# Holding the tokens of a two-layer trunk by parity from the SSD output on, with one 512-column score tile a block of queries

## The chip, the cores and the metric

The kernel runs on one core of a Trainium2 chip. TensorE (PE, with its weight loader PEld) multiplies, VectorE (DVE) and ScalarE (ACT) do the elementwise work, and SyncE (SP) issues the DMAs. The metric is the device time of one execution in microseconds. Before the change it is 1275.34 us, the median of 3 runs from 1275.26 to 1276.29 us. Beside the runs there is the profile of one execution.

## The reference

256 tokens of width 2048 go through two layers; all data are float32. Each layer computes `x <- LayerNorm(alpha * x + (1 + gate) * mixer(x * (1 + scale) + shift))`, where shift, scale and gate come from a condition vector.

- The first mixer is a state-space one (SSD): a projection, a causal convolution of width 4, a scan over the tokens, a SiLU gate, an RMS norm over each of 8 groups of 512 channels, and an output projection from 4096 to 2048. Its output, normalised, also gives one set of keys and values.
- The second mixer is attention with 3 groups of 8 heads of width 128. The groups have windows and dilations (128, 1), (512, 4) and (2048, 16): a query at token t sees the keys t, t - d, t - 2d and so on, down to t - window. Each score is scaled and has a slope times the distance subtracted. The three groups' outputs are merged for each head slot by the weights of their softmax denominators, which is one softmax over the keys of all three groups. A SiLU gate and an output projection from 1024 to 2048 follow.

With 256 tokens, a key in the groups of dilation 4 and 16 is at an even distance from its query.

## The kernel before

Tokens lie in two blocks of 128, `b` = 0 and 1, the first and the second half of the sequence. A projection splits each weight piece of 512 KB into a high and a low part: ACT copies the high one (`split`, line 95) and DVE subtracts the low one (line 97), so that three fast matmuls (or two, in `cm_wide`, lines 145 and 148) make up a float32 product. The attention's own matmuls are plain float32, which TensorE runs as two instructions each.

The order is: the SSD layer (to about 535 us); its output projection in four chunks of 512 columns (`tm_chunk(wout[n], ...)`); keys and values (`cm_wide(wk...)`, `tm_chunk(wv...)`); then `queries(0)`, `attend(0)`, `queries(1)`, `attend(1)`, `z_gate` for two halves of the heads, and the last projection with the final norm. The code is written in program order, and the framework's scheduler puts the instructions of each engine in an order of their own at build time, so that the attention's matmuls stand between those of the next projection. Each engine then runs its instructions in that order.

What the change and the prediction touch:

- `y_tiles` (line 654): while the first chunk of the output projection runs, it transposes the SSD output `y` (token rows) into channel rows, two tiles of 256 tokens to one PSUM bank `pt`. ACT writes the high part into `yhi`, with the norm's weight as scale (line 663), and DVE the low part into `ylo` (line 664). There are 32 such tiles.
- The residual (line 728): the rows of `x` for a block are loaded as `xr`, 128 rows of 512 columns.
- `attend` (line 840): for each of 4 heads and each block `b` of queries, and for each of the 3 groups, one score matmul against the keys of block 0 alone (`b` = 0, 128 columns) or of both blocks (`b` = 1, 256 columns) into a tile `aux` (2 buffers; line 850). DVE makes the bias from slope, distance and mask (line 852) and adds it to the scaled score in `sc0` or `sc1` (line 854). Then come the maximum (line 856), the exponential with its sum on ACT (line 858), the reciprocal and the scaling on DVE (lines 859 and 860), and transposes of the weights in blocks of 128 into PSUM tiles `po` (2 buffers; line 864), which ACT (groups 0 and 2, line 870) or DVE (group 1, line 868) copies into `pT`. After both blocks, six matmuls add up the head's output in another `po` tile (lines 873 and 874), which line 875 copies over the queries of group 0.
- `bias`, a table of 1024 columns: 256 of distances and 3 x 256 of masks.
- `store` (line 947), which writes the output's rows, 512 columns at a time.

Of the kernel before, what the change touches and what calls it, by code (L numbers as in the profile page):

```python
# [9 lines left out]
F32 = mybir.dt.float32  # L10
# [32 lines left out]

CI, CT, CM, NCONST = 0, 128, 256, 640

CD, CA, NBIAS = 0, 256, 256 + 768


@with_exitstack
def trunk(ctx, tc, xT, x, c, par, cst, bias, lnrow, ada, wdt, win, wout, wk, wv, wbin, wbout, out):  # L50
# [32 lines left out]
    ones = cons.tile([P, P], F32, name="ones")  # L83
    V.memset(ones, 1.0)


    def load_piece(src):
        raw = wp.tile([P, 1024], F32, name="raw", bufs=6)
# [197 lines left out]
    with ExitStack() as cA:  # L286
# [367 lines left out]
        def y_tiles(g):  # L654

            for i in range(4):
                ct = 4 * g + i
                if i % 2 == 0:
                    pt = aux.tile([P, 512], F32, name="aux").rearrange("p (i l) -> p i l", i=2)
                for b in range(2):  # L660
                    T.transpose(pt[:, i % 2, b * P:b * P + P], y[g][:, b, i * P:i * P + P], ident)
                w, hi = pv("normg")[:, ct:ct + 1], yhi[g // 4][:, ct % 16, :]
                S.activation(hi, pt[:, i % 2, :], AF.Copy, scale=w)  # L663
                V.scalar_tensor_tensor(ylo[g][:, i, :], pt[:, i % 2, :], w, hi.bitcast(F32),
                                       op0=ALU.mult, op1=ALU.subtract)

        def y_ahead(q):
            if q == 0:
# [45 lines left out]
        for n in range(4):  # L714
            ps = tm_chunk(wout[n], lambda kt: yhi[kt // 16][:, kt % 16, :], lambda kt: ylo[kt // 4][:, kt % 4, :],
                          nk=2 * KT, rate=(1, 4) if n else (0, 1),
                          pre={0: y_ahead, 3: first_weights}.get(n), split_end=4 if n == 3 else 0)
            if n == 0:
                pin[0] = latest[-3].ins
                state[0] = 0  # L720
                queue(pn, cols1[:11])
            if n == 3:
                drain()
            gt = pn.tile([P, 512], F32, name="gt")
            bcast(gt, gated[0], 512 * n)
            for b in range(2):
                xr = pn.tile([P, 512], F32, name="xr", bufs=2)
                nc.sync.dma_start(xr, x[b * P:b * P + P, 512 * n:512 * n + 512])
                residual(n, ps[b], b, (gt, u[b][:, 512 * n:512 * n + 512]), xr)
                if n == 3:  # L730
                    norm.append(moments(b, 4))
                    normalise(b, 0, 256)
                    normalise(b, 256, 512)
# [78 lines left out]
    aux2 = ctx.enter_context(tc.tile_pool(name="aux3", bufs=2, space=PSUM))  # L812
    bs = pc2.tile([P, NBIAS], F32, name="bs", bufs=1)
    nc.sync.dma_start(bs, bias)
    dmat = bs[:, CD:CD + 256]
    amask = bs[:, CA:CA + 768].rearrange("p (g k) -> p g k", g=3)
    R = (0, 1)

    def weigh(n, b, i):
        if b == 0 and i == 0:  # L820
            t = pc2.tile([P, NG, 384], F32, name="pT", bufs=1).rearrange("p g n -> p (g n)")
            lnr[n] = [t[:, 512 * j:512 * j + 512] for j in range(2)]
            for j in range(2):
                bcast(lnr[n][j], lnrow, j * D + 512 * n)
        cs_ = slice(512 * n, 512 * n + 512)
        with tc.issue_after(late):
            V.tensor_tensor(u[b][:, cs_], u[b][:, cs_], lnr[n][i], op=(ALU.mult, ALU.add)[i])
# [12 lines left out]
    def attend(hq, qq):  # L840

        for i in range(4):
            h = 4 * hq + i
            pT = pc2.tile([P, NG, 384], F32, name="pT", bufs=1)
            for b in range(2):
                n = P * (b + 1)
                sc = pc2.tile([P, NG, n], F32, name=f"sc{b}", bufs=1)
                for g in range(NG):
                    pq = aux.tile([P, 512], F32, name="aux")[:, :n]
                    T.matmul(pq, qq[g][:, i, b * P:b * P + P], kv[hq, g][:, i, :n], start=True, stop=True)  # L850
                    bi = pc2.tile([P, 256], F32, name="bi", bufs=2)[:, :n]
                    V.scalar_tensor_tensor(bi, dmat[:, 256 - n:], SLOPES[g * H + h], amask[:, g, 256 - n:],
                                           op0=ALU.mult, op1=ALU.add)
                    V.scalar_tensor_tensor(sc[:, g, :], pq, SCALE, bi, op0=ALU.mult, op1=ALU.add)
                nm = sm.tile([P, 1], F32, name="nm")
                V.tensor_reduce(nm, sc, axis=AX.XY, op=ALU.max, negate=True)
                den = sm.tile([P, 1], F32, name="den")
                S.activation(sc, sc, AF.Exp, bias=nm, accum_out=den)
                V.reciprocal(den, den)
                V.tensor_scalar(sc, sc, den, None, op0=ALU.mult)  # L860
                for g in range(NG):
                    pp = aux2.tile([P, 512], F32, name="po")[:, :n]
                    for kb in range(b + 1):
                        T.transpose(pp[:, kb * P:kb * P + P], sc[:, g, kb * P:kb * P + P], ident)

                    d = pT[:, g, 0:P] if b == 0 else pT[:, g, P:384]
                    if g == 1:
                        V.tensor_copy(d, pp)
                    else:
                        S.activation(d, pp, AF.Copy)  # L870
            po = aux2.tile([P, 512], F32, name="po")[:, :L]
            for g in range(NG):
                T.matmul(po, vt[hq, g][:, 0, i * P:i * P + P], pT[:, g, 0:256], start=g == 0, stop=False)  # L873
                T.matmul(po[:, P:L], vt[hq, g][:, 1, i * P:i * P + P], pT[:, g, 256:384], start=False, stop=g == NG - 1)
            V.tensor_copy(qq[0][:, i, :], po)

    oghi, oglo = ([slots.tile([P, 4, L], F32R, name=f"s{2 * hq + i}") for hq in range(2)] for i in range(2))
# [16 lines left out]
    def hold_in(i, k):  # L894

        j = 4 + 2 * i + k
        if j < 12:
            return (slots if j < 8 else pb).tile([P, 1024], F32R, name=("s" if j < 8 else "b") + str(j))
        if i == 5:
            return pc2.tile([P, 1024], F32R, name="q2")  # L900
        return pc2.tile([P, 1024 + 128 * k], F32R, name=("bs", "pT")[k], bufs=1)[:, :1024]

    qs = [queries(0)]
    attend(0, qs[0])
# [40 lines left out]
        return end  # L945

    def store(b, c):
        nc.sync.dma_start(out[b * P:b * P + P, c], u[b][:, c])

    diag = pc2.tile([P, NG, P], F32, name="sc0", bufs=1)[:, 0, :]  # L950
    for n in range(2):
        last(0, n)
        join(2 + n, ps[n][0], 0)
# [57 lines left out]
def _layout(x, c, ada_w, ada_b, ln_g, ln_b, a_in_w, a_conv_w, a_conv_b, a_dt_bias,  # L1011
            a_A_log, a_D, a_norm_g, a_out_w, kv_w, b_in_w, b_out_w):
    f = np.float32
    par = np.zeros((P, NPAR), f)

    def put(name, a):
        par[:a.shape[0], OFF[name][0]:OFF[name][1]] = a

    ab = ada_b.reshape(2, 3, KT, P)
    put("adab", ab.transpose(3, 0, 2, 1).reshape(P, 96))  # L1020
    put("convw", a_conv_w[0].T.reshape(48, P, 4).transpose(1, 0, 2).reshape(P, 192))
    put("convb", _cm(a_conv_b[0]))
    put("normg", _cm(a_norm_g[0]))
    put("dsk", np.broadcast_to(a_D[0], (P, 64)))
    put("dtb", a_dt_bias[0][:, None])
    put("alog", np.broadcast_to(a_A_log[0], (P, 64)))
    put("lng", _cm(ln_g[0]))
    put("lnb", _cm(ln_b[0]))

    cst = np.zeros((P, NCONST), f)  # L1030
    i = np.arange(P)
    cst[:, CI:CI + 128] = np.eye(P)
    up = (i[:, None] <= i[None, :]).astype(f)
    cst[:, CT:CT + 128] = up
    cst[:, CM:CM + 384] = np.concatenate([up, up, np.ones((P, P), f)], 1)
    bias = np.zeros((P, NBIAS), f)
    delta = 128 + i[:, None] - np.arange(256)[None, :]
    bias[:, CD:CD + 256] = -delta
    for g, (win_, dil) in enumerate(((128, 1), (512, 4), (2048, 16))):
        ok = (delta >= 0) & (delta % dil == 0) & (delta <= win_)  # L1040
        bias[:, CA + 256 * g:CA + 256 * g + 256] = np.where(ok, 0.0, NEG)


    ada = ada_w.reshape(2, D, 3, KT, P).transpose(0, 2, 3, 4, 1)

    w = a_in_w[0]
    z, xs, bb, cc, dt = (w[:, a:b] for a, b in ((0, 4096), (4096, 8192), (8192, 9216), (9216, 10240), (10240, 10304)))
    bc = np.stack([bb.reshape(D, G, P), cc.reshape(D, G, P)], 2).reshape(D, 2048)
    win = _pieces(np.concatenate([bc, xs, z], 1))
    return {  # L1050
        "xT": x[0].T.reshape(KT, P, L).transpose(1, 0, 2), "x": x[0], "c": c, "par": par, "cst": cst, "bias": bias,
        "lnrow": np.stack([ln_g[0], ln_b[0], ln_g[1], ln_b[1]]),
        "ada": ada, "wdt": _dt(dt), "win": win,
        "wout": _pieces(a_out_w[0]), "wk": _pieces(kv_w[:, :3072], 256, 4),
        "wv": _pieces(kv_w[:, 3072:]), "wbin": _pieces(b_in_w[0], 256, 4), "wbout": _pieces(b_out_w[0]),
    }
# [20 lines left out]
```

## Time and profile before

| | |
|---|---|
| median of 3 runs | 1275.34 us |
| span of the profiled execution | 1272.5 us |
| instructions | 19056 |
| HBM read, written | 332.47 MB, 2.18 MB |
| granted TensorE clock, mean | 1.000 |

The span goes from the first to the last instruction of the program; the runs' times also hold what lies around it. In the profile's rows L850 is line 850 of the kernel. A group of instructions shows its line, engine and operation, the tiles written and read by their names in the program, the shape, the count, the busy time, the mean duration of one in ns, and the idle time of the engine just before them with what ended it. Matmuls are pipelined, so that the next one starts before the duration of the last is over. A wait is written as "who <- whom: total us, times, longest us".

### The profile page before, as it was taken

The page shows a single profiled execution, that of the slowest core. Times are in us where ns is not written, and L with a number is a line of the kernel's source. Part 1 is how long each engine was busy: PE and PEld are TensorE (multiplying, and loading weights), DVE is VectorE, ACT ScalarE, POOL GpSimd, SP SyncE. Part 2 cuts the span into 40 slices and gives each one's busy share as a digit, 9 for nine tenths or more (in the row PEclk, how much of TensorE's full clock was granted, in tenths as well). Part 3 has the DMA queues.
Part 4 walks back from the last instruction along what each step waited for, and adds up shares of the span by engine and source line. Part 5 has one row for each costly group of instructions (what it writes and reads, how often), then busy time and mean ns, then how long its engine had stood idle before and what let it go on. Part 6 is the DMA issues. An engine that isn't in the chain of part 4 may idle for free.

```text
span 1272.5 us, 19056 instructions
## 1 busy us (share of the span) xinstructions
PE 1236.6 (97%) x7222; PEld 1078.7 (85%) x7222; DVE 1034.5 (81%) x1498; ACT 704.0 (55%) x1035; POOL 0.2 (0%) x4
## 2 busy tenths in 40 slices
PE   4999999999999999999999999999999999999997
PEld 4889989899898999778888788888878888888885
DVE  6999986999998878869776678878888867758876
ACT  3655577757677777764344445434345645444731
POOL 0000000000000000000000000000000000000000
PEclk9999999999999999999999999999999999999999
DMA  9999968696866546468988469989998774463751
GB/s 386 423 420 422 420 211 298 224 341 234 314 247 208 157 149 216 167 216 292 338 282 282 160 195 353 357 328 348 357 381 316 235 240 130 127 204 100 222 192 66
DMA packets 80588, 335.89 MB, mean 264 GB/s; under 512 B 9105, under 2 KB 9329, under 8 KB 67697
## 3 DMA queue, kind: packets, MB, share of 16 engines
q1 hardware_dynamic: 80496, 334.69, 73.5%
q8 instruction: 56, 0.92, 0.3%
q14 instruction: 36, 0.29, 0.1%
HBM read 332.47 MB, written 2.18 MB: 263 GB/s over the span
## 4 chain that ended last, share of the span: by engine, by line
PE 85%; DVE 8%; DMA 3%; issue 2%; ACT 1%; SPq 0%; DVEq 0%; ACTq 0%
PE acc L145 14%; PE acc L171 12%; PE acc L170 12%; PE acc L169 12%; PE acc L148 7%; PE acc L123 7%; PE acc L121 7%; PE acc L122 7%; DVE araw L247 2%; DVE wlo L97 2%; PE py L608 2%; PE aux L850 1%; DMA araw<-in_ada 1%; DMA raw<-in_wk 1%; PE po L873 1%
## 5 line engine op out<-in xcount | busy, mean ns | idle before, releaser
L95 ACT ACTIVATE whi<-raw 128x1024 fp32r<-128x1024 f32 x392 | 411.3, 1058 | 369.4 <-PE acc L171 127.3
L97 DVE TENSOR_TENSOR wlo<-raw,whi 128x1024 fp32r<-128x1024 f32 x392 | 473.3, 1220 | 140.3 <-ACT whi L95 139.5
L145 PE MATMUL acc<-actT,whi 128*128 128x512 f32 x896 | 285.9, 398 | 0.0
L170 PE MATMUL acc<-wlo,actT 128*128 128x512 f32 x688 | 269.7, 392 | 1.1 <-DVE wlo L97 0.9
L169 PE MATMUL acc<-whi,actT 128*128 128x512 f32 x688 | 266.7, 394 | 0.9 <-ACT actT L663 0.9
L121 PE MATMUL acc<-actT,whi 128*128 128x256 f32 x768 | 217.4, 285 | 17.5 <-ACT actT L398 17.3
L247 DVE SCALAR_TENSOR_TENSOR araw<-araw,cb__72 128x2048 f32<-128x2048 f32 x96 | 219.2, 2284 | 14.6 <-DMA araw<-in_ada 14.5
L123 PE MATMUL acc<-actT,wlo 128*128 128x256 f32 x768 | 214.9, 285 | 4.9 <-DVE wlo L97 4.9
L122 PE MATMUL acc<-actT,whi 128*128 128x256 f32 x768 | 217.1, 284 | 0.0
L148 PEld LDWEIGHTS acc<-actT,wlo 128*128 128x128 f32 x896 | 167.0, 188 | 42.1 <-DVE wlo L97 5.0
L148 PE MATMUL acc<-actT,wlo 128*128 128x256 f32 x896 | 180.9, 282 | 1.9 <-DVE wlo L97 1.2
L171 PE MATMUL acc<-whi,actT 128*128 128x512 f32 x432 | 168.7, 391 | 0.0
L121 PEld LDWEIGHTS acc<-actT,whi 128*128 128x128 f32 x768 | 147.7, 193 | 18.7 <-ACT actT L398 17.5
L170 PEld LDWEIGHTS acc<-wlo,actT 128*128 128x128 f32 x688 | 129.3, 188 | 29.1 <-DVE wlo L97 3.4
L123 PEld LDWEIGHTS acc<-actT,wlo 128*128 128x128 f32 x768 | 146.5, 193 | 6.0 <-DVE wlo L97 5.8
L169 PEld LDWEIGHTS acc<-whi,actT 128*128 128x128 f32 x688 | 128.7, 188 | 26.7 <-ACT actT L663 1.4
L122 PEld LDWEIGHTS acc<-actT,whi 128*128 128x128 f32 x768 | 148.1, 193 | 0.3
L145 PEld LDWEIGHTS acc<-actT,whi 128*128 128x128 f32 x896 | 137.5, 189 | 0.3
L171 PE MATMUL acc<-whi,ylo 128*128 128x512 f32 x256 | 100.5, 393 | 0.0
L171 PEld LDWEIGHTS acc<-whi,actT 128*128 128x128 f32 x432 | 81.1, 188 | 16.6
L171 PEld LDWEIGHTS acc<-whi,ylo 128*128 128x128 f32 x256 | 48.0, 188 | 9.7
L319 DVE SCALAR_TENSOR_TENSOR cacc<-acc,prm,cacc 128x253 f32<-128x253 f32 (+2 forms) x96 | 42.1, 474 | 6.1 <-ACT cacc L316 5.8
(251 smaller groups left out, 1110.2 us busy)
## 6 DMA issues: line engine op xcount, KB each, us to landing
araw<-in_ada SPq DMA_DIRECT2D x96, 1024.0 KB, 7.5
raw<-in_win SPq DMA_DIRECT2D x160, 512.0 KB, 5.6
raw<-in_wout SPq DMA_DIRECT2D x64, 512.0 KB, 4.8
raw<-in_wbin SPq DMA_DIRECT2D x64, 512.0 KB, 4.3
raw<-in_wv SPq DMA_DIRECT2D x48, 512.0 KB, 5.4
raw<-in_wk SPq DMA_DIRECT2D x48, 512.0 KB, 7.7
cbc<-cumd SPq DMA_DIRECT2D x16, 512.0 KB, 5.2
raw<-in_wbout SPq DMA_DIRECT2D x16, 512.0 KB, 4.7
```

Of the source, the lines that this page charges most:

```text
L95: copied.append(S.activation(hi, raw, AF.Copy))
L97: latest.append(V.tensor_tensor(lo, raw, hi.bitcast(F32), op=ALU.subtract))
L121: T.matmul(o, hi[:, k, c_], ahi[:, kt, :], start=first, stop=False, skip_group_check=True)
L122: T.matmul(o, hi[:, k, c_], alo[:, kt, :], start=False, stop=False, skip_group_check=True)
L123: T.matmul(o, lo[:, k, c_], ahi[:, kt, :], start=False, stop=kt == k1 - 1, skip_group_check=True)
L145: T.matmul(ps[n], hi[:, k, n * P:n * P + P], xp[:, kt], start=kt == 0, stop=False, skip_group_check=True)
L148: T.matmul(ps[n][:, 0, :], lo[:, k, n * P:n * P + P], xhi[:, kt, :], start=False, stop=kt == KT - 1, skip_group_check=True)
L169: T.matmul(o, h_, hi[:, k, :], start=kt == k0, stop=False, skip_group_check=part)
L170: T.matmul(o, h_, lo[:, k, :], start=False, stop=False, skip_group_check=part)
L171: end = T.matmul(o, l_, hi[:, k, :], start=False, stop=kt == k1 - 1, skip_group_check=part)
L247: V.scalar_tensor_tensor(raw, raw, 1.0, cb_, op0=ALU.mult, op1=ALU.mult, accum_out=mod[layer][:, ct, j:j + 1])
L319: V.scalar_tensor_tensor(acc[:, o:], ps[:, :L - o], w[:, j:j + 1], acc[:, o:], op0=ALU.mult, op1=ALU.add)
```

## The change

Three things change.

First, `y_tiles` writes `yhi` and `ylo` with the tokens sorted by parity: columns 0 to 127 are the even tokens and 128 to 255 the odd ones. The transposes into PSUM stay as they are; the two copies read them with a step of two. From there on a "block" is a parity, down to the output: the residual's rows of `x` are loaded, and the output's rows stored, with a step of two rows (`rows`).

Second, in `attend` the groups of dilation 4 and 16 take keys of the query's own parity alone, 128 of them, and the group of dilation 1 takes all 256. So both blocks of queries have 256 + 128 + 128 columns of scores, in one PSUM bank; three matmuls fill it and one addition adds the bias. The biases are made once a head, for both blocks, in one tile `bi` of 640 columns (384 for group 0, whose two blocks take two different thirds of each side, and 128 for each of the others). The four transposes of a block go into one `po` tile, of which ACT copies the first half and DVE the second. The output is six matmuls, two of 256 columns and four of 128.

Third, the `bias` table has 384 columns of distances and 640 of masks, and some tiles have other sizes (`pT` 1024 columns in place of 1152, `sc0` and `sc1` 512 in place of 384 and 768).

```diff
-                w, hi = pv("normg")[:, ct:ct + 1], yhi[g // 4][:, ct % 16, :]
-                S.activation(hi, pt[:, i % 2, :], AF.Copy, scale=w)
-                V.scalar_tensor_tensor(ylo[g][:, i, :], pt[:, i % 2, :], w, hi.bitcast(F32),
-                                       op0=ALU.mult, op1=ALU.subtract)
+                w = pv("normg")[:, ct:ct + 1]
+                hi, lo = (t.rearrange("p (r j) -> p r j", r=2) for t in (yhi[g // 4][:, ct % 16, :], ylo[g][:, i, :]))
+                by_parity = pt[:, i % 2, :].rearrange("p (j r) -> p r j", r=2)
+                S.activation(hi, by_parity, AF.Copy, scale=w)
+                V.scalar_tensor_tensor(lo, by_parity, w, hi.bitcast(F32), op0=ALU.mult, op1=ALU.subtract)
...
+    def rows(t, b):
+        return t.rearrange("(j r) n -> r j n", r=2)[b]
...
-                nc.sync.dma_start(xr, x[b * P:b * P + P, 512 * n:512 * n + 512])
+                nc.sync.dma_start(xr, rows(x, b)[:, 512 * n:512 * n + 512])
...
-            pT = pc2.tile([P, NG, 384], F32, name="pT", bufs=1)
+            pT = pc2.tile([P, 4, 2, P], F32, name="pT", bufs=1)
+            bi = pc2.tile([P, 640], F32, name="bi", bufs=1)
+            for g, c_ in enumerate((slice(0, 384), slice(384, 512), slice(512, 640))):
+                V.scalar_tensor_tensor(bi[:, c_], dmat if g == 0 else dmat[:, P:2 * P], SLOPES[g * H + h], gmask[:, c_],
+                                       op0=ALU.mult, op1=ALU.add)
             for b in range(2):
-                n = P * (b + 1)
-                sc = pc2.tile([P, NG, n], F32, name=f"sc{b}", bufs=1)
-                for g in range(NG):
-                    pq = aux.tile([P, 512], F32, name="aux")[:, :n]
-                    T.matmul(pq, qq[g][:, i, b * P:b * P + P], kv[hq, g][:, i, :n], start=True, stop=True)
-                    bi = pc2.tile([P, 256], F32, name="bi", bufs=2)[:, :n]
-                    V.scalar_tensor_tensor(bi, dmat[:, 256 - n:], SLOPES[g * H + h], amask[:, g, 256 - n:],
-                                           op0=ALU.mult, op1=ALU.add)
-                    V.scalar_tensor_tensor(sc[:, g, :], pq, SCALE, bi, op0=ALU.mult, op1=ALU.add)
+                sc = pc2.tile([P, 512], F32, name=f"sc{b}", bufs=1)
+                pq = aux.tile([P, 512], F32, name="aux")
+                qb = slice(b * P, b * P + P)
+                T.matmul(pq[:, 0:L], qq[0][:, i, qb], kv[hq, 0][:, i, :], start=True, stop=True)
+                for g in range(1, NG):
+                    T.matmul(pq[:, (g + 1) * P:(g + 2) * P], qq[g][:, i, qb], kv[hq, g][:, i, qb], start=True, stop=True)
+                two = "p (a n) -> p a n"
+                bias_b = (bi[:, P:640].rearrange(two, a=2) if b == 0 else
+                          bass.AP(tensor=bi.tensor, offset=bi.offset, ap=[bi.ap[0], [384, 2], [1, 256]]))
+                V.scalar_tensor_tensor(sc.rearrange(two, a=2), pq.rearrange(two, a=2), SCALE, bias_b,
+                                       op0=ALU.mult, op1=ALU.add)
...
-                for g in range(NG):
-                    pp = aux2.tile([P, 512], F32, name="po")[:, :n]
-                    for kb in range(b + 1):
-                        T.transpose(pp[:, kb * P:kb * P + P], sc[:, g, kb * P:kb * P + P], ident)
-
-                    d = pT[:, g, 0:P] if b == 0 else pT[:, g, P:384]
-                    if g == 1:
-                        V.tensor_copy(d, pp)
-                    else:
-                        S.activation(d, pp, AF.Copy)
+                pp = aux2.tile([P, 512], F32, name="po")
+                for k in range(4):
+                    T.transpose(pp[:, k * P:k * P + P], sc[:, k * P:k * P + P], ident)
+                pp = pp.rearrange("p (k n) -> p k n", k=4)
+                S.activation(pT[:, 0:2, b, :], pp[:, 0:2, :], AF.Copy)
+                V.tensor_copy(pT[:, 2:4, b, :], pp[:, 2:4, :])
             po = aux2.tile([P, 512], F32, name="po")[:, :L]
-            for g in range(NG):
-                T.matmul(po, vt[hq, g][:, 0, i * P:i * P + P], pT[:, g, 0:256], start=g == 0, stop=False)
-                T.matmul(po[:, P:L], vt[hq, g][:, 1, i * P:i * P + P], pT[:, g, 256:384], start=False, stop=g == NG - 1)
+            head = slice(i * P, i * P + P)
+            for b in range(2):
+                T.matmul(po, vt[hq, 0][:, b, head], pT[:, b].rearrange("p b n -> p (b n)"), start=b == 0, stop=False)
+            for g in range(1, NG):
+                for b in range(2):
+                    T.matmul(po[:, b * P:b * P + P], vt[hq, g][:, b, head], pT[:, g + 1, b, :], start=False,
+                             stop=g == NG - 1 and b == 1)
...
-        nc.sync.dma_start(out[b * P:b * P + P, c], u[b][:, c])
+        nc.sync.dma_start(rows(out, b)[:, c], u[b][:, c])
```

More of the change, by code (lines that the diff above doesn't have):

```diff
@@ L44 @@
 CI, CT, CM, NCONST = 0, 128, 256, 640
-CD, CA, NBIAS = 0, 256, 256 + 768
+CD, CG, NBIAS = 0, 384, 384 + 384 + 256
 @with_exitstack
@@ L814, in trunk @@
     nc.sync.dma_start(bs, bias)
-    dmat = bs[:, CD:CD + 256]
-    amask = bs[:, CA:CA + 768].rearrange("p (g k) -> p g k", g=3)
+    dmat = bs[:, CD:CD + 384]
+    gmask = bs[:, CG:CG + 640]
     R = (0, 1)
@@ L820, in weigh @@
         if b == 0 and i == 0:
-            t = pc2.tile([P, NG, 384], F32, name="pT", bufs=1).rearrange("p g n -> p (g n)")
+            t = pc2.tile([P, 1024], F32, name="pT", bufs=1)
             lnr[n] = [t[:, 512 * j:512 * j + 512] for j in range(2)]
@@ L843, in attend @@
             h = 4 * hq + i
-            pT = pc2.tile([P, NG, 384], F32, name="pT", bufs=1)
-            for b in range(2):
-                n = P * (b + 1)
-                sc = pc2.tile([P, NG, n], F32, name=f"sc{b}", bufs=1)
-                for g in range(NG):
-                    pq = aux.tile([P, 512], F32, name="aux")[:, :n]
-                    T.matmul(pq, qq[g][:, i, b * P:b * P + P], kv[hq, g][:, i, :n], start=True, stop=True)
-                    bi = pc2.tile([P, 256], F32, name="bi", bufs=2)[:, :n]
-                    V.scalar_tensor_tensor(bi, dmat[:, 256 - n:], SLOPES[g * H + h], amask[:, g, 256 - n:],
-                                           op0=ALU.mult, op1=ALU.add)
-                    V.scalar_tensor_tensor(sc[:, g, :], pq, SCALE, bi, op0=ALU.mult, op1=ALU.add)
+            pT = pc2.tile([P, 4, 2, P], F32, name="pT", bufs=1)
[3 more added lines that the diff above has]
+                                       op0=ALU.mult, op1=ALU.add)
+            for b in range(2):
+                sc = pc2.tile([P, 512], F32, name=f"sc{b}", bufs=1)
[9 more added lines that the diff above has]
+                                       op0=ALU.mult, op1=ALU.add)
                 nm = sm.tile([P, 1], F32, name="nm")
-                V.tensor_reduce(nm, sc, axis=AX.XY, op=ALU.max, negate=True)
+                V.tensor_reduce(nm, sc, axis=AX.X, op=ALU.max, negate=True)
                 den = sm.tile([P, 1], F32, name="den")
@@ L900, in hold_in @@
             return pc2.tile([P, 1024], F32R, name="q2")
-        return pc2.tile([P, 1024 + 128 * k], F32R, name=("bs", "pT")[k], bufs=1)[:, :1024]
+        return pc2.tile([P, 1024], F32R, name=("bs", "pT")[k], bufs=1)
     qs = [queries(0)]
@@ L947, in store @@
     def store(b, c):
-        nc.sync.dma_start(out[b * P:b * P + P, c], u[b][:, c])
-    diag = pc2.tile([P, NG, P], F32, name="sc0", bufs=1)[:, 0, :]
+        nc.sync.dma_start(rows(out, b)[:, c], u[b][:, c])
+    diag = pc2.tile([P, 512], F32, name="sc0", bufs=1)[:, :P]
     for n in range(2):
@@ L1036, in _layout, with mask @@
     bias = np.zeros((P, NBIAS), f)
[L1037 to L1041, printed above, removed]
+    same = 2 * (i[:, None] - i[None, :])
+    near = np.concatenate([same + 1, same, same - 1], 1)
+    bias[:, CD:CD + 384] = -near
+    def mask(delta, win_, dil):
+        return np.where((delta >= 0) & (delta % dil == 0) & (delta <= win_), 0.0, NEG)
+    bias[:, CG:CG + 384] = mask(near, 128, 1)
+    bias[:, CG + 384:CG + 512] = mask(same, 512, 4)
+    bias[:, CG + 512:CG + 640] = mask(same, 2048, 16)
     ada = ada_w.reshape(2, D, 3, KT, P).transpose(0, 2, 3, 4, 1)
```

## The prediction

> **What bounds the kernel now.** I read the page first: the share of each engine and the chain that ended last. Then I read the stage that the change cuts, with the busy time by stretch, the waits of TensorE's weight loader and the rows in order of time.
>
> ```profile
> span 1272.5 us, 19056 instructions
> PE 1236.6 (97%) x7222; PEld 1078.7 (85%) x7222; DVE 1034.5 (81%) x1498; ACT 704.0 (55%) x1035; POOL 0.2 (0%) x4
> ...
> PE 85%; DVE 8%; DMA 3%; issue 2%; ACT 1%; SPq 0%; DVEq 0%; ACTq 0%
> ```
>
> TensorE is busy for 97% of the span and is 85% of the chain. The profiled execution has a span of 1272.5 us; the median of the runs is 1275.34, so 2.8 us lie around the span. I make the sum against the span and add those 2.8 us again.
>
> The attention is interleaved with projections: `attend(0)` with the matmuls of `queries(1)`, `attend(1)` with those of `z_gate`. Here are the stretches from the first score matmul to the last gate projection (us, then busy us of PE, its loader, DVE, ACT, POOL, the granted clock, the DMA share and rate):
>
> ```profile
> 1062.00:1110.00 48.00, 48.00 (x289) 41.45 (x288) 39.51 (x101) 25.00 (x49) 0.00 (x0) 1.00 0.36 105
> 1110.00:1150.00 40.00, 40.00 (x232) 34.94 (x231) 21.27 (x22) 17.44 (x21) 0.00 (x0) 1.00 0.68 206
> 1150.00:1216.00 66.00, 66.00 (x394) 56.76 (x393) 57.01 (x118) 41.28 (x70) 0.00 (x0) 1.00 0.55 169
> ```
>
> PE has no visible gap in 154 us; DVE has 36 us free and ACT 70. The loader's waits from 995 to 1216 us (total, times, longest):
>
> ```profile
> PEld po L864 <- ACT pT L870: 4.0, 13, 0.4
> PEld acc L148 <- DVE wlo L97: 0.7, 1, 0.7
> PEld po L864 <- DVE sc L860: 0.2, 1, 0.2
> ```
>
> Only the transposes wait, for a `po` buffer that a copy must empty, and only 0.3 us a time. The long softmax chain costs TensorE 0.2 us in all. So this stage is a sum of TensorE's own work.
>
> A matmul's duration overlaps the next one's, so I price by start to start:
>
> ```profile
> 1071.62 0.60 PE L864 MATMUL po<-cc,sc 128*128 128x128 f32 x4
> 1072.05 0.60 PE L850 MATMUL aux<-s,q 128*128 128x256 f32 x2
> 1072.48 0.43 PE L864 MATMUL po<-cc,sc 128*128 128x128 f32 x2
> ...
> 1073.49 0.60 PE L873 MATMUL po<-pT,s 128*128 128x256 f32 x2
> 1073.92 0.38 PE L874 MATMUL po<-pT,s 128*128 128x128 f32 x2
> 1074.14 0.60 PE L873 MATMUL po<-pT,s 128*128 128x256 f32 x2
> ```
>
> Four transposes take 0.43 us. One 256-column float32 matmul is two instructions and takes 0.43 (L850 and L873 alike); one of 128 columns takes 0.22. So a unit, one instruction of 128 columns, is 0.108 us.
>
> How much stall is in the stage? It begins at the first row below and ends at the last; between are 26 groups of projection matmuls without attention:
>
> ```profile
> 995.32 0.62 PE L145 MATMUL acc<-actT,whi 128*128 128x512 f32 x2
> ```
> ```profile
> 1193.69 0.62 PE L145 MATMUL acc<-actT,whi 128*128 128x512 f32 x2
> ...
> 1211.80 0.40 PE L145 MATMUL acc<-actT,whi 128*128 128x512 f32 x1
> ```
> ```profile
> 1215.98 0.40 PE L169 MATMUL acc<-whi,s 128*128 128x512 f32 x1
> ```
> ```profile
> L145 PE MATMUL acc<-actT,whi 128*128 128x512 f32 x512 | 165.3, 400 | 0.0
> ...
> L864 PE MATMUL po<-cc,sc 128*128 128x128 f32 x72 | 14.2, 281 | 0.0
> L850 PE MATMUL aux<-s,q 128*128 128x256 f32 x40 | 11.1, 379 | 0.0
> ```
>
> The stage is 1215.98 - 995.32 = 220.7 us. A group (two of L145, two of L148) takes (1211.80 - 1193.69) / 26 = 0.697 us, and 512 of L145 make 256 groups: 178.3 us. That leaves 42.4 us for attention. By the code a head has score matmuls of 3 x 128 and 3 x 256 columns, two instructions each (18 units), nine transposes (9 units; 8 heads make the x72) and output matmuls of 3 x (256 + 128) columns (18 units): 45 units, 4.86 us, and 38.9 for 8 heads. So 3.5 us of the stage are stall, 0.7 of it the projection's wait for DVE.
>
> **The change part by part.**
>
> *TensorE in the attention.* A head gets two score tiles of 256 + 128 + 128 columns (16 units), eight transposes (8) and output matmuls of 2 x 256 + 4 x 128 columns (16): 40 units instead of 45. The number of weight loads for scores and outputs stays at 12 matmuls a head. 5 units x 0.108 x 8 heads = **4.3 us**, all on the path, since PE is full and more projection work stands behind it: the gate projections run on for 22 us after the last output matmul (1193.69 to 1215.98).
>
> *Stall.* Taken from `po` are 7 tiles a head now (six of transposes, one output); then 3. The 3.5 - 0.7 = 2.8 us of attention stall may stay whole or go whole. 32 of 56 `po` tiles go, which by share would be 1.6 us, but each copy that remains moves more. I take **0.7 us**, between none and 2.8.
>
> *DVE and ACT.* From the same stretch (count, busy us, mean ns, idle before):
>
> ```profile
> L854 DVE SCALAR_TENSOR_TENSOR sc<-aux,bi 128x256 f32<-128x256 f32 x24 | 9.8, 413 | 0.4 <-PE po L864 0.3
> ...
> L856 DVE TENSOR_REDUCE nm<-sc 128x1 f32<-128x768 f32 x8 | 7.5, 942 | 0.0
> ...
> L854 DVE SCALAR_TENSOR_TENSOR sc<-aux,bi 128x128 f32<-128x128 f32 x24 | 6.4, 284 | 3.1 <-PE aux L850 2.5 <-PE po L864 0.3
> ...
> L856 DVE TENSOR_REDUCE nm<-sc 128x1 f32<-128x384 f32 x8 | 4.3, 542 | 0.0
> ```
> ```profile
> L858 ACT ACTIVATE sc<-sc,nm 128x768 f32<-128x768 f32 x8 | 7.5, 935 | 2.5 <-DVE nm L856 2.5
> L870 ACT ACTIVATE pT<-po 128x256 f32<-128x256 f32 x16 | 6.0, 377 | 4.9 <-PE po L864 4.9
> ...
> L858 ACT ACTIVATE sc<-sc,nm 128x384 f32<-128x384 f32 x8 | 4.9, 611 | 4.8 <-DVE nm L856 4.8
> L870 ACT ACTIVATE pT<-po 128x128 f32<-128x128 f32 x16 | 4.4, 273 | 15.3 <-PE po L864 15.2
> ```
>
> On DVE, an element of L854 costs (413 - 284) / 128 = 1.01 ns, so 512 columns take 0.67 us (estimate), and 384 take 0.54. A head before: three biases and three scores of each size, priced alike, 6 x (0.284 + 0.413) = 4.18, and reductions of 1.48, together 5.66. After: biases 0.54 + 2 x 0.28, scores 2 x 0.67, reductions of 512 at 0.68 each: 3.80. That is 15 us less for 8 heads. On ACT a head goes from 1.55 + 2 x (0.273 + 0.377) = 2.85 to 2 x 0.72 + 2 x 0.377 = 2.19, 5 us less. I count both at **nothing**: TensorE waited on neither but for the stalls above. Their relief is the cover for the one new dependence, that four transposes wait for one 512-column softmax. Of that chain the last score addition, the reduction and the exponential take 0.67 + 0.68 + 0.72 = 2.1 us, where the second block now takes 0.41 + 0.94 + 0.94 = 2.3; what follows them is the same or shorter. Its successor in PE's queue, a projection matmul, would wait behind it.
>
> *The transposes of y.* The 32 copies that fill `yhi` and `ylo` now read PSUM with a step of two elements; the writes stay contiguous. No row of the trace reads with such a step.
>
> ```profile
> L664 DVE SCALAR_TENSOR_TENSOR ylo<-aux,prm,actT x32: 471/477/485, 536.5 to 582.6; 128x256 fp32r<-128x256 f32 x32
> ```
> ```profile
> L663 ACT ACTIVATE actT<-aux,prm x32: 452/464/475, 534.9 to 581.9; 128x256 fp32r<-128x256 f32 x32
> ```
> ```profile
> PEld acc L169 <- ACT actT L663: 1.4, 2, 0.9
> PE acc L169 <- ACT actT L663: 0.9, 2, 0.5
> ...
> PE aux L661 <- DVE ylo L664: 0.7, 2, 0.4
> ```
> ```profile
> 545.00:575.00 30.00, 30.00 (x150) 23.92 (x149) 19.86 (x29) 16.78 (x30) 0.00 (x0) 1.00 0.64 202
> 575.00:585.00 10.00, 10.00 (x50) 8.22 (x49) 10.00 (x14) 5.57 (x9) 0.00 (x0) 1.00 0.82 284
> ```
>
> The low end is no change: about 1 ns an element on DVE and (377 - 273) / 128 = 0.81 on ACT look like one element at a time, with nothing gained from neighbours, and no reason gives a gain. The high end that I price is every element at twice its time: 0.26 us a tile on DVE and 0.21 on ACT. TensorE waits for the first four tiles in turn, so 4 x 0.47 = 1.9 us there. Between 545 and 575 us DVE has 10.1 us free and would get some 20 tiles x 0.26 = 5.2 us, hidden. From 575 on DVE is full, and the last 6 tiles add 1.6 us. Together 3.5 us. I take nothing, since the one-at-a-time slopes are the nearest rows.
>
> [...]
>
> *DMA.* The rows of `x` and `out` go by parity.
>
> ```profile
> xr<-in_x SPq DMA_DIRECT2D x8, 256.0 KB, 5.5
> ...
> out<-u SPq DMA_DIRECT2D x8, 256.0 KB, 2.4
> ```
>
> Each stays 128 runs of 2 KB (512 float32), in the same place in SP's queue; only the step between runs doubles. The loads are hidden under a chunk of the output projection; of the eight stores only the last is bare. I take nothing; a tenth on the last store would be 0.2 us. The bias table keeps its 512 KB.
>
> Sum: 4.3 + 0.7 = 5.0 us less. Span 1267.5, time **1270.3 us**.
>
> **The rivals.**
>
> *All stall goes.* The 2.8 us of attention stall vanish with the smaller number of `po` tiles: 4.3 + 2.8 = 7.1 less, **1268.2**. For it speaks that the `po` wait is the only frequent one; against it that such waits were 0.3 us each and scheduling leaves some.
>
> *Stepped PSUM reads at twice the time:* 5.0 - 3.5 = 1.5 less, **1273.8**. For it: TensorE already waits on L663 and L664 at the start. Against: the slopes.
>
> *A wait takes the place.* If TensorE meets each of the 16 groups of four transposes 0.3 us too early, as it meets `po` now, 4.8 us come back: **1275.1**. Against: the softmax cost it 0.2 us in all, and DVE and ACT have less to do.
>
> *Stepped reads at three times or more, the slower side.* With n times the element's time the price is 3.5 (n - 1), and past n = 3 DVE's free 10.1 us are used up and 5.2 (n - 1) - 10.1 is added. It decides at about n = 3.1, where the price is past 5.0 + 2.5 us; at n = 4 it is 10.5 + 5.5 = 16.0 and the time **1286.3**.
>
> **How the numbers follow.** A measurement of this kernel tells about 0.2%, 2.55 us, from no change. Chances: forecast 0.60, all stall gone 0.10, twice the time 0.10, a wait in its place 0.10, three times and more 0.10. The first two are faster: 0.70; the next two are the same: 0.20; the last is slower: 0.10. The range reaches from a little under the second case, 1267.4, to just above the fourth, 1275.2, and leaves out the slower case and the tails.
>
> **What would show it.** Right: transposes x64 in place of x72; the stage from the first projection of queries to the first output projection 215.7 us instead of 220.7; the same group pace of 0.697; L663 and L664 near 464 and 477 ns. Wrong: those two rows longer, with PE waiting on them around 535 to 545 us; PEld waiting for the scaled scores in front of the transposes; gaps in PE between 1062 and 1190 us; or the order of the instructions outside the attention shifted so that projections wait for their weights.

## The result and the profile after

The kernel after the change takes 1270.14 us (median of 5 runs, 1268.58 to 1272.54) where the kernel before, beside it, takes 1276.29 (5 runs, 1275.26 to 1276.87). The ratio is 0.9954, 95% interval 0.9943 to 0.9964: faster by 0.46%. The forecast was 1270.3 us, from 5.0 us of gain; the gain is 6.2 us by the medians and 5.9 by the ratio.

The page of the kernel after (lines are moved: L99 and L101 are the split's two parts, L149 and L152 the projection's matmuls, L858 and L860 the scores, L874 the transposes, L876 and L877 their copies, L881 and L884 the output matmuls):

```profile
span 1270.8 us, 18959 instructions
PE 1233.8 (97%) x7214; PEld 1077.7 (85%) x7214; DVE 1025.5 (81%) x1442; ACT 697.8 (55%) x1017; POOL 0.2 (0%) x4
...
PE 84%; DVE 8%; DMA 5%; issue 1%; ACT 1%; SPq 0%; DVEq 0%; ACTq 0%
```

TensorE still holds the chain. But this profiled execution is only 1.7 us shorter than the one of before (1270.8 against 1272.5), and not 6. It took 1272.54 us, the longest of the five runs. So the stages must be compared one by one. First TensorE's matmuls of the stage (count, busy us, mean ns, idle before):

```profile
L149 PE MATMUL acc<-actT,whi 128*128 128x512 f32 x512 | 163.7, 398 | 0.0
L152 PE MATMUL acc<-actT,wlo 128*128 128x256 f32 x512 | 102.0, 280 | 1.5 <-DVE wlo L101 1.5
L858 PE MATMUL aux<-s,q 128*128 128x256 f32 x32 | 9.9, 390 | 0.0
L874 PE MATMUL po<-cc,sc 128*128 128x128 f32 x64 | 9.5, 274 | 0.0
```

The transposes are 64 in place of 72, the projection has its 512 matmuls as before, and there is something new: 1.5 us in which TensorE waits for low parts. Here are the ends of the stage, from the first projection of queries to the first output projection:

```profile
997.54 0.62 PE L149 MATMUL acc<-actT,whi 128*128 128x512 f32 x2
```
```profile
1214.62 0.40 PE L173 MATMUL acc<-whi,s 128*128 128x512 f32 x1
```

The stage is 217.1 us, where it was 220.7. Of that, 178.3 are the projection's 256 groups and 40 x 8 x 0.108 = 34.6 the attention's units; 4.2 are left as stall. The loader's waits in it:

```profile
PEld acc L152 <- DVE wlo L101: 2.4, 2, 1.4
PEld po L881 <- ACT pT L876: 0.9, 3, 0.5
PEld aux L858 <- DVE sc L864: 0.7, 3, 0.3
```

2.4 us are two waits for low parts, neither of them in the attention. Here is the longer one in order of time, in the first queries:

```profile
1025.14 0.69 DVE L832 TENSOR_TENSOR u<-u,pT 128x512 f32<-128x512 f32 x1 [1.17 <-DMA pT<-in_lnrow]
...
1025.75 1.22 DVE L101 TENSOR_TENSOR wlo<-raw,whi 128x1024 fp32r<-128x1024 f32 x1
...
1027.02 0.30 PEld L152 LDWEIGHTS acc<-actT,wlo 128*128 128x128 f32 x2 [1.43 <-DVE wlo L101]
```

DVE stands for 1.17 us before an instruction whose rows of the first norm have not come, the low part is queued behind it, and TensorE waits for the low part. Code and place are the same before the change; there such waits were 0.7 us. What belongs to the attention has become small: the 4.0 us of waits for `po` before the transposes are gone, and 0.9 before the output matmuls and 0.7 before the scores have come.

And the rest of the 1.7 us? The stage gives 3.6, and two places ahead of it take back 2.2. The transposes for keys and values, before and after:

```profile
L745 PE MATMUL aux<-cc,u x32: 270/272/328, 719.5 to 758.7; 128*128 128x128 f32 x32
```
```profile
L750 PE MATMUL aux<-cc,u x32: 270/272/328, 720.2 to 760.9; 128*128 128x128 f32 x32
```

The first is 0.6 us later (that lateness is there already at the first transposes of `y`, 535.1 us against 534.5, ahead of anything changed), the last 2.2. Between them the granted clock, the third column from the end of a row with the engines' busy time, was not full. Before and after, from 722 to 730 us:

```profile
722.00:730.00 8.00, 7.30 (x33) 5.51 (x33) 6.40 (x27) 4.46 (x9) 0.00 (x0) 1.00 0.68 262
```
```profile
722.00:730.00 8.00, 7.75 (x28) 5.61 (x26) 5.87 (x24) 3.81 (x6) 0.00 (x0) 0.79 0.70 262
```

A clock of 0.79 over 8 us is, as an estimate, 8 x 0.21 = 1.7 us of TensorE's work lost. A clock below full is not the change's alone: the mean over a run is 0.998 to 1.000 in the five runs of the kernel after, 0.997 to 1.000 in the 23 of the kernel before beside the first experiments, and 1.000 in the profile of before. Where the clock fell in the runs without a profile is not shown. So: -3.6 for the stage, +0.6 and +1.6 ahead of it, and -0.3 behind it.

### The profile page after: what moved, and what is told of

It reads as the page before. It is cut to its first block, busy times and chain, and to the rows that moved or that the text cites. A ratio compares the mean times of both kernels' runs of the same rounds, so it can differ in the third digit from the quotient of the medians.

```text
span 1270.8 us, 18959 instructions
## 1 busy us (share of the span) xinstructions
PE 1233.8 (97%) x7214; PEld 1077.7 (85%) x7214; DVE 1025.5 (81%) x1442; ACT 697.8 (55%) x1017; POOL 0.2 (0%) x4
## 3 DMA queue, kind: packets, MB, share of 16 engines
HBM read 332.47 MB, written 2.18 MB: 263 GB/s over the span
## 4 chain that ended last, share of the span: by engine, by line
PE 84%; DVE 8%; DMA 5%; issue 1%; ACT 1%; SPq 0%; DVEq 0%; ACTq 0%
PE acc L149 13%; PE acc L175 12%; PE acc L174 12%; PE acc L173 12%; PE acc L127 7%; PE acc L152 7%; PE acc L125 7%; PE acc L126 7%; DMA araw<-in_ada 2%; DMA raw<-in_wk 2%; PE py L612 2%; DVE araw L251 2%; DVE wlo L101 2%; DVE cacc L323 1%; DMA raw<-in_wv 1%
## 5 line engine op out<-in xcount | busy, mean ns | idle before, releaser
L99 ACT ACTIVATE whi<-raw 128x1024 fp32r<-128x1024 f32 x392 | 412.1, 1058 | 391.1 <-PE acc L175 134.5
L101 DVE TENSOR_TENSOR wlo<-raw,whi 128x1024 fp32r<-128x1024 f32 x392 | 473.8, 1221 | 152.4 <-ACT whi L99 146.7
L149 PE MATMUL acc<-actT,whi 128*128 128x512 f32 x896 | 284.3, 397 | 0.0
L127 PE MATMUL acc<-actT,wlo 128*128 128x256 f32 x768 | 215.1, 285 | 4.9 <-DVE wlo L101 4.9
L152 PEld LDWEIGHTS acc<-actT,wlo 128*128 128x128 f32 x896 | 166.8, 188 | 44.4 <-DVE wlo L101 6.7
L152 PE MATMUL acc<-actT,wlo 128*128 128x256 f32 x896 | 178.0, 280 | 3.2 <-DVE wlo L101 2.5
L149 PEld LDWEIGHTS acc<-actT,whi 128*128 128x128 f32 x896 | 137.3, 189 | 0.2
```

Of the source, the lines that this page charges most:

```text
L99: copied.append(S.activation(hi, raw, AF.Copy))
L101: latest.append(V.tensor_tensor(lo, raw, hi.bitcast(F32), op=ALU.subtract))
L127: T.matmul(o, lo[:, k, c_], ahi[:, kt, :], start=False, stop=kt == k1 - 1, skip_group_check=True)
L149: T.matmul(ps[n], hi[:, k, n * P:n * P + P], xp[:, kt], start=kt == 0, stop=False, skip_group_check=True)
L152: T.matmul(ps[n][:, 0, :], lo[:, k, n * P:n * P + P], xhi[:, kt, :], start=False, stop=kt == KT - 1, skip_group_check=True)
```

## The experiments

The theory (A): the gain is TensorE work taken out of the attention, 4.3 us, and somewhat less stall. The rivals: (B) it comes from fewer and shorter instructions on DVE and ACT and from fewer `po` tiles; (C) part of it comes from the new order of the tokens, or the stepped reads take part of it back. The kernel before took 1276.29, 1275.48 and 1277.65 us in the three sets of runs, so kernels of different sets are compared by their ratio to it.

### The order alone

The hunks of the change in `y_tiles`, of `xr` and of `store` are put into the kernel before; its attention stays.

> The kernel before with the parity order alone: the stepped PSUM reads of y, the stepped rows of x and of the output, and the attention left as it was. (Its masks then stand for the sequence's order while the tokens are in parity order, so it computes another attention of the same amount of work.) Theory A, the gain is TensorE work taken out of the attention: no gain here, 1275.3 to 1277.0 as before, L663 and L664 at 464 and 477 ns. Rival C, part of the gain comes from the new order itself: at least 2 us less than before. If stepped reads cost twice the time: 3.5 us more than before.

Measured: 1275.44 us (median of 11 runs) beside 1275.48 (23 runs) of before; ratio 0.9999, interval 0.9990 to 1.0007. The stepped reads, on DVE and on ACT:

```profile
L670 DVE SCALAR_TENSOR_TENSOR ylo<-aux,prm,actT 128x256 fp32r<-128x256 f32 x32 | 14.4, 478 | 3.1 <-ACT actT L669 3.0
L669 ACT ACTIVATE actT<-aux,prm 128x256 fp32r<-128x256 f32 x32 | 13.8, 465 | 9.5 <-PE aux L665 9.5
```

They take what they took without a step (477 and 464 ns), to 1 ns. Rival C falls in both directions: the order by itself, stepped DMAs included, neither gains nor costs more than about 1 us, the width of the interval to either side.

### The attention alone

The reverse: the kernel after with those hunks undone.

```diff
-                by_parity = pt[:, i % 2, :].rearrange("p (j r) -> p r j", r=2)
-                S.activation(hi, by_parity, AF.Copy, scale=w)
...
+                S.activation(hi, pt[:, i % 2, :], AF.Copy, scale=w)
...
-                nc.sync.dma_start(xr, rows(x, b)[:, 512 * n:512 * n + 512])
+                nc.sync.dma_start(xr, x[b * P:b * P + P, 512 * n:512 * n + 512])
```

> The kernel after with the tokens in the sequence's order again: y, x and the output read and written without a step, the new attention kept. (Its masks then belong to another order of the tokens; the amount of work is that of the kernel after.) Theory A: 1269 to 1271.5, as after; the stage from the first projection of queries to the first output projection 216 us without stalls of the weights. Rival C: 1272 or more.

Measured: 1269.91 us (6 runs), ratio 0.9964 (0.9952 to 0.9976). The ends of its stage:

```profile
996.35 0.62 PE L149 MATMUL acc<-actT,whi 128*128 128x512 f32 x2
```
```profile
1211.45 0.40 PE L173 MATMUL acc<-whi,s 128*128 128x512 f32 x1
```

215.1 us, with no wait for low parts in the first queries: 5.6 less than the 220.7 of before, and 0.9 less than the 216 expected. The whole gain of the stage is in the attention.

### The units put back

```diff
+                if b == 1:
+                    T.matmul(pq[:, 2 * P:3 * P], qq[1][:, i, qb], kv[hq, 1][:, i, qb], start=True, stop=True)
...
+                if b == 1:
+                    T.transpose(pp[:, 3 * P:4 * P], sc[:, 3 * P:4 * P], ident)
...
+            T.matmul(po[:, 0:P], vt[hq, 0][:, 0, head], pT[:, 0, 0, :], start=True, stop=True)
```

> The kernel after with 5 units a head of TensorE work put back as repeats that change no value: one score matmul of 128 columns, one transpose and one output matmul of 128 columns more a head. Theory A: 40 units x 0.108 = 4.3 us more than after, about 1274.4. Rival B, the gain comes from fewer and shorter instructions on DVE and ACT and from fewer po tiles: 1270 to 1271, as after, since those stay as they are.

Measured: 1274.92 us (11 runs), ratio 0.9999 (0.9990 to 1.0007): the whole gain is lost again, with DVE, ACT and the `po` tiles as the change left them. Its stage, and the repeats in it (L862, L878, L884):

```profile
996.23 0.62 PE L149 MATMUL acc<-actT,whi 128*128 128x512 f32 x2
```
```profile
1216.53 0.40 PE L173 MATMUL acc<-whi,s 128*128 128x512 f32 x1
```
```profile
L862 PE MATMUL aux<-s,q 128*128 128x128 f32 x16 | 3.1, 275 | 0.0
L878 PE MATMUL po<-cc,sc 128*128 128x128 f32 x8 | 2.2, 272 | 0.0
L884 PE MATMUL po<-pT,s 128*128 128x128 f32 x8 | 1.6, 287 | 0.0
L884 PE MATMUL po<-pT,b 128*128 128x128 f32 x8 | 1.6, 279 | 0.0
```

16 + 8 + 16 = 40 instructions of 128 columns make the stage 220.3 us, 5.2 more than the 215.1 of the attention alone. 0.7 of that is a wait for a low part that the other profile did not have, so 4.5 are the repeats: 0.11 each. Theory A said 4.3. This is the run that decides against B as the main cause; the part of B that the `po` tiles could have comes below.

### The biases made twice

```diff
-            for g, c_ in enumerate((slice(0, 384), slice(384, 512), slice(512, 640))):
-                V.scalar_tensor_tensor(bi[:, c_], dmat if g == 0 else dmat[:, P:2 * P], SLOPES[g * H + h], gmask[:, c_],
-                                       op0=ALU.mult, op1=ALU.add)
             for b in range(2):
+                for g, c_ in enumerate((slice(0, 384), slice(384, 512), slice(512, 640))):
+                    V.scalar_tensor_tensor(bi[:, c_], dmat if g == 0 else dmat[:, P:2 * P], SLOPES[g * H + h],
+                                           gmask[:, c_], op0=ALU.mult, op1=ALU.add)
```

> The kernel after with the biases made once for each block of queries again, not once a head: 24 DVE instructions more, 8 x 1.11 = 8.9 us of DVE work. Theory A: 1269.5 to 1271, within 0.7 us of after, since DVE has 36 us free in this stretch. Rival B: 2 us or more above after.

Measured: 1268.92 us (5 runs), ratio 0.9950 (0.9938 to 0.9962), where the kernel after has 0.9954; the time is a little below the 1269.5 to 1271 expected. DVE does have the work:

```profile
L853 DVE SCALAR_TENSOR_TENSOR bi<-bs 128x384 f32<-128x384 f32 x16 | 8.8, 549 | 0.3 <-DMA bs<-in_bias 0.3
L853 DVE SCALAR_TENSOR_TENSOR bi<-bs 128x128 f32<-128x128 f32 x32 | 8.2, 282 | 0.0
```

Half of these 17 us are the addition. The stage is 215.2 us. DVE's time in this stretch is free, as its 36 us of idle time said.

### Nine po tiles a head

```diff
-                pp = aux2.tile([P, 512], F32, name="po")
                 for k in range(4):
-                    T.transpose(pp[:, k * P:k * P + P], sc[:, k * P:k * P + P], ident)
-                pp = pp.rearrange("p (k n) -> p k n", k=4)
-                S.activation(pT[:, 0:2, b, :], pp[:, 0:2, :], AF.Copy)
-                V.tensor_copy(pT[:, 2:4, b, :], pp[:, 2:4, :])
+                    pp = aux2.tile([P, 512], F32, name="po")[:, :P]
+                    T.transpose(pp, sc[:, k * P:k * P + P], ident)
+                    if k < 2:
+                        S.activation(pT[:, k, b, :], pp, AF.Copy)
+                    else:
+                        V.tensor_copy(pT[:, k, b, :], pp)
```

> The kernel after with each transpose in a po tile of its own and a copy of its own: 9 po tiles a head in place of 3 (7 before the change), 64 copies in place of 32; TensorE's units stay at 40 a head. If po tiles make the stall: 2.0 us of stall at 24 tiles and 2.9 at 56 give 3.3 at 72, so 1 to 1.5 us above after, about 1271. If the stall hangs on something else, such as the change between kinds of matmul: within 0.5 us of after.

Measured: 1272.14 us (5 runs), ratio 0.9965 (0.9951 to 0.9979), where the kernel after beside it has 0.9952 (0.9940 to 0.9964): 0.7 us slower by the medians, less than the 1 to 1.5 expected, and the intervals overlap, so the times alone don't tell. The stage does, 216.7 us against 215.1, and its loader waits for copies again:

```profile
PEld po L874 <- ACT pT L876: 2.4, 9, 0.4
PEld aux L858 <- DVE sc L864: 0.5, 2, 0.3
PEld acc L152 <- DVE wlo L101: 0.4, 1, 0.4
```

Here are the profiles with their stages. The rest is the stage without 178.3 us of projection and without the units at 0.108 us; from it the loader's wait for the projection's low parts is taken off.

| kernel | po tiles in all | units a head | stage, us | rest | wait for low parts | attention's stall |
|---|---|---|---|---|---|---|
| before | 56 | 45 | 220.7 | 3.5 | 0.7 | 2.8 |
| the order alone | 56 | 45 | 220.1 | 2.9 | 0.2 | 2.7 |
| after | 24 | 40 | 217.1 | 4.2 | 2.4 | 1.8 |
| after, again | 24 | 40 | 215.7 | 2.9 | 0.7 | 2.2 |
| the attention alone | 24 | 40 | 215.1 | 2.2 | 0.0 | 2.2 |
| the biases twice | 24 | 40 | 215.2 | 2.4 | 0.7 | 1.7 |
| the units put back | 24 | 45 | 220.3 | 3.1 | 0.7 | 2.4 |
| nine po tiles | 72 | 40 | 216.7 | 3.9 | 0.4 | 3.5 |

The stall goes with the number of `po` tiles: 1.7 to 2.4 us at 24, 2.7 to 2.8 at 56, 3.5 at 72 (3.3 was expected). The last column is a little too small where a low part came late, because the loader's wait counts some 0.2 us more than TensorE loses by it. In the kernel after, the pairs of L149 around the wait of 1.43 us start at 1025.40 and 1027.36, 1.96 us for a group of 0.70, so 1.26 are lost. With what TensorE loses, which is an estimate from this one wait for all of them, the stall is 1.8 to 2.6 us at 24 tiles, 2.9 to 3.0 at 56 and 3.6 at 72. The repeats of the units put back come to 4.7 us by the same reckoning. The order stays, but the step from 56 to 24 may be as small as 0.3 us. The number of copies changes with the tiles, so the two are not told apart.

### A step of 16 in place of 2

```diff
-                hi, lo = (t.rearrange("p (r j) -> p r j", r=2) for t in (yhi[g // 4][:, ct % 16, :], ylo[g][:, i, :]))
-                by_parity = pt[:, i % 2, :].rearrange("p (j r) -> p r j", r=2)
+                hi, lo = (t.rearrange("p (r j) -> p r j", r=16) for t in (yhi[g // 4][:, ct % 16, :], ylo[g][:, i, :]))
+                by_parity = pt[:, i % 2, :].rearrange("p (j r) -> p r j", r=16)
```

> The kernel after with y read from PSUM with a step of 16 elements, 64 bytes, in place of 2 (the tokens then stand in another order than the masks say). If reads of PSUM by DVE and ACT do not care for the step: the two rows stay at 464 and 478 ns and the time at 1270. [...]

Measured: 1270.50 us (4 runs), ratio 0.9947 (0.9933 to 0.9961). The rows do not move:

```profile
L670 DVE SCALAR_TENSOR_TENSOR ylo<-aux,prm,actT x32: 474/478/485, 539.0 to 585.1; 128x256 fp32r<-128x256 f32 x32
```
```profile
L669 ACT ACTIVATE actT<-aux,prm x32: 452/465/475, 537.4 to 584.5; 128x256 fp32r<-128x256 f32 x32
```

### The kernel after once more, and the first norm's rows loaded early

> The kernel after once more, for another profile beside the next three. Theory A: 1268.5 to 1271.5; the stage from the first projection of queries to the first output projection 215.2 us plus whatever the projection waits for its weights there (0 to 2 us), as the two runs before it with this attention show (215.1 and 215.2).

Measured: 1271.40 us (5 runs) beside 1277.65 (9 runs) of before, ratio 0.9952 (0.9940 to 0.9964). The gain of 0.5% is the same a second time.

The last kernel takes up the wait for low parts that this work met: DVE waits in the first queries for rows of the first norm, and the next low part waits behind it. Its edit:

```diff
-        if b == 0 and i == 0:
-            t = pc2.tile([P, 1024], F32, name="pT", bufs=1)
...
+        if b == 1 and i == 1 and n < 2:
+            lnr_load(n + 2)
+    def lnr_load(n):
+        if n % 2 == 0:
+            t = pc2.tile([P, 1024], F32, name="pT", bufs=1)
+            lnr[n] = [t[:, 512 * j:512 * j + 512] for j in range(2)]
+        else:
+            lnr[n] = [pc2.tile([P, 512], F32, name=f"sc{j}", bufs=1) for j in range(2)]
...
+    for n in range(2):
+        lnr_load(n)
```

> The kernel after with the rows of the first norm's weight and bias loaded two chunks ahead, chunks 1 and 3 into the idle score tiles, so that DVE does not wait for them between the first queries' weights (9.7 us of DVE waits, and 0 to 2 us of TensorE's waits for the low parts, differing from run to run). If those waits are what makes the runs of after differ: no stall in the first queries, 0.5 to 1.5 us below after, about 1269. If not: as after.

Measured: 1270.11 us (5 runs), ratio 0.9944 (0.9932 to 0.9957), 1.3 us below the kernel after beside it by the medians. DVE's waits for these rows fall from 8.9 us to 2.3 (after once more, then this one):

```profile
DVE u L832 <- DMA pT<-in_lnrow: 8.9, 8, 3.0
```
```profile
DVE u L827 <- DMA sc<-in_lnrow: 1.6, 1, 1.6
...
DVE u L827 <- DMA pT<-in_lnrow: 0.7, 2, 0.4
```

No low part comes late in its first queries, and its stage is 215.1 us. But two of the other kernels, the attention alone and the step of 16, had none late either without this edit, and the intervals overlap. That it beats the kernel after is likely and not shown.

## Why the prediction was right, point by point

- **TensorE's units, 4.3 us, all on the path.** Right. The transposes are x64, the projection's groups kept their pace (39 of them from 1186.75 to 1213.92 us, 0.697 each), and 40 instructions put back cost 4.5 us of the stage and the whole gain of the time.
- **Stall, 0.7 us between none and 2.8.** Right in size, as far as the table can tell: 2.7 to 2.8 us became 1.7 to 2.4. The size was a choice inside the bounds, not a sum, so that it came out is partly luck. The mechanism was right, the wait of the transposes for a `po` tile, since nine tiles a head brought it back, 2.4 us in nine times; tiles or copies is not told apart. "All stall goes" did not happen: small waits of the output matmuls for `pT` and of the scores for an `aux` tile took its place.
- **DVE and ACT at nothing.** The sizes were right: the kernel after has scores of 16 x 0.682, reductions of 16 x 0.675 and biases of 8 x (0.549 + 2 x 0.281), 30.6 us, in place of 45.3, 14.7 less where 15 were forecast. In busy time all of DVE fell by 9.0 us (1034.5 to 1025.5) and all of ACT by 6.2 (704.0 to 697.8). DVE's durations overlap in part: before the change they add up to about 1125 us. The 8.5 us of biases put back cost nothing. The shorter scores, reductions and copies were not put back by themselves; that they gave nothing either follows from the units put back, which lost the gain with all of them in place.
- **"A wait takes the place."** It did not: the four transposes wait for the scaled scores in no row of the loader's waits. The new waits named above are 1.6 us in six times, not 4.8, and the stage became shorter with them.
- **Stepped PSUM reads at nothing.** Right; steps of 2 and of 16 are both free here, with 478 ns on DVE and 465 on ACT for either and 477 and 464 without a step. With that both rivals of slow reads fall: no run shows a read at twice its time, which the high end assumed. This holds for reads by DVE and ACT; no run here steps a matmul's own access to PSUM.
- **DMA at nothing.** Right by the order alone, 1275.44 against 1275.48.
- **What lies around the span.** The prediction took 2.8 us, from the median of the runs and the span of one other execution, and let it stay the same. By the spans listed with the runs it is 2.1 to 2.2 us for the kernel before and for the order alone, and 1.7 to 1.9 for every kernel with the new attention, the units put back too. So some 0.35 us of the gain lie outside the span. What in the new attention's code does that is not shown.
- **The sum and where it was to be seen.** The time was met, 1270.14 for 1270.3, but that it was met so closely is luck: the forecast counted from 1275.34, and beside the result the kernel before took 1276.29. The gain, 5.9 us by the ratio with an interval of 4.6 to 7.3, holds the 5.0 of the sum, and 0.35 more are those outside the span; the rest of the difference is within the scatter. The range was wide, too, and reached almost to no change, so the stage says more. It was forecast at 215.7 us: 215.1 to 215.7 in four of the five profiles with 40 units a head and 24 `po` tiles whose stages are given above. The fifth is the profile of the change itself, at 217.1 for its late low parts. What the prediction did not price is how much single executions differ by such waits and by the clock: its 1267.5 us of span stand against 1270.8 in the profile and 1266.8 to 1270.8 over the five runs.

## What to carry to other kernels

Where one engine is full and the others wait for it (here TensorE, busy for 97% of the span), count its instructions in the stage that changes, price them by start to start and not by their durations (0.43 us against 0.60 for a score matmul of 256 columns), and check that count by subtracting it from the stage's length: what is left is the stall (3.5 of 220.7 us here), and no more than that can be won there by taking away waits. A profile of a single execution can hide a gain of 0.5% behind a late load or a dip of the clock (here the spans of the two profiles differ by 1.7 us and the medians by 6.2), so compare the stage's ends and not the spans. An experiment that puts back only the suspected work, with the same values, tells more than one that takes something away.

## What the runs showed of the hardware that was not expected

- DVE and ACT read float32 from PSUM with steps of 2 and 16 elements at the pace of contiguous reads: 478 and 465 ns for 256 columns against 477 and 464. The forecast had taken this from slopes alone and priced twice the time as the high end.
- In the profile of the kernel after, the granted clock was 0.79 of full speed between 722 and 730 us. It stood at 0.50 from 723.8 to 727.2 us, and at 1.00 from 722 to 723 and from 727.2 to 730. In the 7 us from 715 to 722 us TensorE was busy for 6.03 us in both kernels, and the kernel before kept the full clock. In the 3.4 us just ahead of the dip, as long as the dip itself, TensorE was busy for 2.18 us; in the kernel before it was busy for 2.17 of the 3.4 us from 719.6 to 723.0, and the clock stayed at 1.00 after it (723.0 to 726.4). So TensorE's busy time ahead of it does not tell the two apart, and what lowered the clock is not shown by these runs.

```profile
715.00:722.00 7.00, 6.03 (x28) 4.80 (x27) 5.44 (x16) 4.79 (x8) 0.00 (x0) 1.00 0.02 9
```
```profile
715.00:722.00 7.00, 6.03 (x27) 4.52 (x25) 5.44 (x16) 5.42 (x9) 0.00 (x0) 1.00 0.01 4
```

The first row is of the kernel after, the second of the kernel before.
